# Three of the four sums of weight blocks in a seven-product SwiGLU made by accumulating transfers from GpSimd's queue instead of by VectorE

## The chip, the cores and the metric

The kernel runs on one core of a Trainium2 chip. The metric is device time of the program in microseconds (us), the median of several runs. Times inside the profile are counted from the start of the profiled execution's span. TensorE is PE in the rows (PEld its weight loads), VectorE is DVE, ScalarE is ACT, GpSimd is POOL, SyncE is SP; SP issues the ordinary transfers.

## The reference

A decoder trunk of two layers on 512 tokens of width 1024, in float32. Layer 0 mixes with stick-breaking attention, layer 1 with a dilated attention. Behind each mixer stands a SwiGLU with 2816 hidden columns, and this is the part that matters here:

```python
def _swiglu(h, w_gate, w_up, w_down):
    return (jax.nn.silu(h @ w_gate) * (h @ w_up)) @ w_down
...
    h = h + _swiglu(_rmsnorm(h, norm_ffn[layer]), w_gate[layer], w_up[layer], w_down[layer])
```

## The kernel before, in words

Every matmul runs in three passes: a weight block of 128x512 numbers is split into a high part (`whi`, written by ACT at L306 in a narrower format) and the rest (`wlo`, written by DVE at L307); the activations are split likewise, and high x high, high x rest and rest x high are added up in PSUM. So each weight block costs one load from `wflat` (SP, L243), one ACT instruction and one DVE instruction before PE can use it. `whi` and `wlo` live in a ring of four tiles, `w2hi` and `w2lo` in one of three more; a split may run up to six blocks ahead of PE.

**The SwiGLU.** The 2816 hidden columns are 22 blocks of 128. Blocks 0 and 1 are computed plainly (`gu`). The other twenty go in ten pairs, g = 1 to 10 (`product`, L964). For a pair, gate and up are the rows of a 2x2 block matrix (row: gate or up; column: first or second half of the 1024 inputs), the tokens are its two columns, and seven products P1, P2, P6, P5, P7, P4, P3 replace eight. P1, P2 and P4 take a weight block as it is; P5, P6, P7 and P3 take sums of blocks. With the blocks named w(row, half), and signs folded in elsewhere: s1 = w(1,0)+w(1,1) for P5, s2 = s1+w(0,0) for P6, s3 = w(1,0)+w(0,0) for P7, s4 = s2+w(0,1) for P3. DVE makes them in `split`: s1 at L280, s2 at L281, s3 at L287, s4 at L291, once for each of the twenty blocks of a layer. The tiles `sum` hold s1, s2 and s4, `raw` (or `raw2`) the loaded blocks; s3 is added in place.

Between the products stand the blocks of the down projection (`dn`). It is done in parts: part 0 covers hidden blocks 0 and 1, its eight output blocks follow P7, P4 and P3 of pair 1 (three, three and two of them); the later parts cover four hidden blocks each. A `dn` block accumulates in one of the two PSUM banks `pj`, and DVE adds it to the residual stream `H` (`residual`, L752); the third `dn` in a row can start only when the first one's bank has been read there.

**What sets the order.** The code is written as calls; a scheduler places the instructions on the engines' queues, and each queue is run in order. `weight_stream` lists the blocks to load (`units`) and the splits (`ops`), `Weights.load` issues loads as the `raw` rings allow, `Weights.split` makes sums and splits, and `get` hands a block to PE and splits ahead. Of each queue the head alone can run: what stands behind a waiting instruction waits too.

The entry of the SwiGLU also has VectorE work of its own: the rows' norm (L471 to L482), the token sums for the seven products (`tk`, `XT`, L899 to L914), and the gating of blocks 0 and 1 (L875 to L881, with L877 on GpSimd). GpSimd multiplies `up` by the norm (L951) twice a pair.

Of the kernel before, what the change touches and what calls it, by code (L numbers as in the profile page):

```python
# [79 lines left out]
def weight_stream():  # L80


    units, ops, place = [], [], {}

    def unit(key, width):
        if key not in place:
            place[key] = len(units)
            units.append((key, width))
        return place[key]

    for layer in range(2):
        for kind, i in mixer_order():
            r = (kind, layer, i)
            for j in range(4):
                gain = None
                if layer == 1 and kind == "qk":
                    which, part = (j % 2, j // 2) if crossed(r) else (j // 2, j % 2)
                    gain = ("k", (G_MIX1, G_KV)[which] + 4 * part)
                elif layer == 1 and kind == "v":
                    gain = ("v", G_KV + 2 * j)  # L100
                ops.append((kind, "mix", ("raw", unit((*r, j), 512)), gain))
        for step in ffn_order():
            if step[0] == "gu":
                for j in range(4):
                    ops.append(("gu", "mix", ("raw", unit(("gu", layer, step[1], j), 512)), None))
            elif step[0] == "dn":
                a, b = PARTS[step[1]]
                held = layer == 1 and step[1] == len(PARTS) - 1
                ops.append(("dn", "held" if held else "ffn",
                            ("raw", unit(("dn", layer, *step[1:]), 128 * (b - a))), None))  # L110
            else:
                for i in range(2):
                    f = 2 * step[1] + i
                    w = lambda r, c: unit(("w", layer, f, r, c), 512)
                    what = {"P1": lambda: ("raw", w(0, 0)), "P2": lambda: ("raw", w(0, 1)),
                            "P6": lambda: ("s2", w(1, 0), w(1, 1), w(0, 0)), "P5": lambda: ("s1",),
                            "P7": lambda: ("s3", w(1, 0), w(0, 0)), "P4": lambda: ("raw", w(1, 1)),
                            "P3": lambda: ("s4", w(0, 1))}[step[2]]()
                    ops.append(("pr", "ffn", (*what, i) if what[0][0] == "s" else what, None))
    return units, ops  # L120


def pack_weights(w_qkv_a, w_o_a, w_kv, w_q_b, w_o_b, w_gate, w_up, w_down):

    def cols(m, n):
        k = m.shape[0] // 128
        return m[:, 128 * n:128 * n + 128].reshape(k, 128, 128).transpose(1, 0, 2).reshape(128, -1)

    def block(m, r):
        return m[:, 256 * r:256 * r + 256].reshape(8, 128, 256).transpose(1, 0, 2).reshape(128, -1)  # L130

    wq = [w_qkv_a[0][:, :D], w_q_b[0]]
    wk = [w_qkv_a[0][:, D:2 * D], w_kv[:, :D]]
    wv = [w_qkv_a[0][:, 2 * D:], w_kv[:, D:]]
    wo = [w_o_a[0], w_o_b[0]]
    parts = []
    for key, width in weight_stream()[0]:
        kind, l = key[:2]
        if kind == "qk":
            t = cross(key, [cols(wq[l], key[2]), cols(wk[l], key[2])])[key[3]]  # L140
        elif kind == "v":
            t = block(wv[l], key[2])[:, 512 * key[3]:512 * key[3] + 512]
        elif kind == "o":
            g, q = O_ORDER[4 * key[2] + key[3]]
            t = block(wo[l], g)[:, 512 * q:512 * q + 512]
        elif kind == "gu":
            t = cross(key, [cols(w_gate[l], key[2]), cols(w_up[l], key[2])])[key[3]]
        elif kind == "w":
            _, _, f, r, c = key
# [40 lines left out]
class Weights:  # L190
# [8 lines left out]
    def __init__(self, tc, pool, wflat, gains):  # L199
        self.tc, self.nc, self.pool, self.w, self.gains = tc, tc.nc, pool, wflat, gains  # L200
        self.units, self.ops = weight_stream()
        self.offs = np.concatenate([[0], np.cumsum([128 * n for _, n in self.units])]).tolist()
        last = {}
        for n, op in enumerate(self.ops):
            for u in self.used(op):
# [5 lines left out]
        for n, op in enumerate(self.ops):  # L211
            for u in self.used(op):
                first.setdefault(u, n)

        self.uring, self.oring = [], []
        q = 0
# [11 lines left out]
        self.live = dict.fromkeys(self.size, 0)  # L228
        self.pools = {"raw": pool, "w": pool}
        self.rt, self.wt, self.sums = {}, {}, {}  # L230
        self.nload = self.nsplit = self.nget = 0

    @staticmethod
    def used(op):
        what = op[2]
        return {"raw": what[1:], "s2": what[1:4], "s1": (), "s3": what[1:3], "s4": what[1:2]}[what[0]]

    def load(self):
        u = self.nload
        ring = self.uring[u]  # L240
        _, n = self.units[u]
        t = self.pools[ring].tile([128, 512], F, name=ring, bufs=self.size[ring])
        self.nc.sync.dma_start(t[:, :n], bass.AP(  # L243
            tensor=self.w.tensor, offset=self.w.offset + self.offs[u], ap=[[n, 128], [1, n]]))
        self.rt[u] = t[:, :n]
        self.live[ring] += 1
        self.nload += 1

# [19 lines left out]
    def split(self):  # L268
# [3 lines left out]
        for v in self.used(self.ops[u]):  # L272
            while self.nload <= v:
                self.load()
        r = [self.rt[v] for v in self.used(self.ops[u])]
        if what[0] == "raw":
            v = r[0]
        elif what[0] == "s2":
            s1, s2 = (self.pools["sum"].tile([128, 512], F, name="sum", bufs=4) for _ in range(2))
            nc.vector.tensor_add(s1, r[0], r[1])  # L280
            nc.vector.tensor_add(s2, s1, r[2])  # L281
            self.sums[what[-1]] = (s1, s2)
            v = s2
        elif what[0] == "s1":
            v = self.sums[what[-1]][0]
        elif what[0] == "s3":
            nc.vector.tensor_add(r[0], r[0], r[1])  # L287
            v = r[0]
        else:
            v = self.sums.pop(what[-1])[1]  # L290
            nc.vector.tensor_add(v, v, r[0])  # L291
        n = v.shape[1]
        ring = self.oring[u]
        if ring == "held":
# [10 lines left out]
            nc.gpsimd.tensor_mul(v3, v3, g.unsqueeze(2).to_broadcast([128, n // m, m]))  # L305
        nc.scalar.activation(hi[:, :n], v, AF.Copy)  # L306
        nc.vector.tensor_sub(lo[:, :n], v, hi[:, :n].bitcast(F))  # L307
        self.wt[u] = (hi, lo)
        self.live[ring] += 1
        for v in self.ends.get(u, ()):  # L310
# [5 lines left out]
    def get(self, kind):  # L316
        u = self.nget
        if u and self.oring[u - 1] != "held":
            self.live[self.oring[u - 1]] -= 1
        ahead = self.AHEAD[self.ops[u][1]]  # L320
        while self.nsplit <= min(u + ahead, len(self.ops) - 1) and (
                self.nsplit <= u or self.ready(self.nsplit, u)):
            self.split()
# [5 lines left out]
def trunk(ctx, tc, xg, wflat, cst_d, cs_d, outT):  # L329
# [777 lines left out]


    W.kept = X
    W.kept0 = next(u for u, (key, _) in enumerate(W.units) if key[:3] == ("dn", 1, len(PARTS) - 1))  # L1110
    for c in range(8):
        norm_chunk(c, G_MIX0, None)
    mixer(0, 0, G_FFN0)
# [33 lines left out]
```

## Time and profile before

| what | value |
|---|---|
| runs | 1217.39, 1218.11, 1220.19 us; median 1218.11 |
| profiled execution | 1217.75 us, of which its span 1216.0 us |
| PE busy | 1187.4 us (98%) |
| DVE busy | 1021.9 us (84%) |
| ACT / POOL busy | 698.8 us (57%) / 173.2 us (14%) |
| transfers | 138.30 MB, all issued by SP apart from 1.34 MB of instructions |
| SwiGLU of layer 0 | from about 250 to 602 us in the span |
| SwiGLU of layer 1 | from about 855 to 1200 us |

PE's busy time is modelled from pipelined matmuls. So whether PE waits is read from the idle time ahead of single matmuls and from the pace of a run of them, not from the percentage. An engine other than PE costs time only where a matmul waits for it.

### The profile page before, as it was taken

How to read it: one execution, taken by the hardware profiler on the slowest of the kernel's cores; microseconds unless marked ns; L12 is line 12 of the kernel's file. 1: busy time of each engine (PE TensorE's matmuls, PEld its weight loads, DVE VectorE, ACT ScalarE, POOL GpSimd, SP SyncE). 2: the span in 40 equal slices, each digit the busy share in tenths (PEclk: the TensorE clock that was granted, in tenths of full speed). 3: DMA queues.
4: the chain of work that ended last, by engine and by line, in shares of the span. 5: the costliest groups of instructions: out<-in, count | busy, mean ns of one | idle time of the engine just before them, and what ended most of it. 6: DMA issues, size and time to landing. Idle time of an engine off the chain costs nothing.

```text
span 1216.0 us, 21067 instructions
## 1 busy us (share of the span) xinstructions
PE 1187.4 (98%) x7481; PEld 1060.8 (87%) x7481; DVE 1021.9 (84%) x1833; ACT 698.8 (57%) x1332; POOL 173.2 (14%) x237
## 2 busy tenths in 40 slices
PE   9999999998999999999999999999899999999997
PEld 7989988877999999999788888887789999999996
DVE  6799999899997878787768899788999878787865
ACT  6667676674554444454467677767655454544443
POOL 0000000002100000014225443110011000000111
PEclk9999999999999999999999999999999999999998
DMA  7654644224243323333145556551343433343122
GB/s 262 175 146 115 155 116 119 61 84 159 88 122 94 115 87 114 96 105 87 35 129 144 156 134 176 142 137 53 95 140 105 121 97 112 89 117 88 47 62 70
DMA packets 74361, 138.30 MB, mean 114 GB/s; under 512 B 9617, under 2 KB 13713, under 8 KB 74257
## 3 DMA queue, kind: packets, MB, share of 16 engines
q1 hardware_dynamic: 74256, 136.97, 40.1%
q8 instruction: 59, 0.97, 0.3%
q14 instruction: 46, 0.37, 0.1%
HBM read 106.00 MB, written 2.10 MB: 89 GB/s over the span
## 4 chain that ended last, share of the span: by engine, by line
PE 85%; DVE 6%; DMA 3%; ACT 2%; issue 2%; POOL 1%; SPq 0%; POOLq 0%; DVEq 0%; ACTq 0%
PE pj L388 38%; PE z L388 30%; PE t L388 11%; PE av L388 3%; PE t L704 3%; DMA mov<-hl 1%; DVE wlo L307 1%; DVE H L752 1%; DMA raw<-wflat 1%; DMA rp<-rp 0%; DMA H<-xg 0%; DVE sum L280 0%; DVE w2lo L307 0%; DVE X L422 0%; DVE sum L281 0%
## 5 line engine op out<-in xcount | busy, mean ns | idle before, releaser
L306 ACT ACTIVATE whi<-raw 128x512 fp32r<-128x512 f32 (+1 forms) x290 | 178.2, 620 | 139.1 <-PE pj L388 50.2
L307 DVE TENSOR_TENSOR wlo<-raw,whi 128x512 fp32r<-128x512 f32 (+1 forms) x290 | 203.4, 709 | 25.0 <-ACT whi L306 22.6
L388 PE MATMUL pj<-VO,whi 128*128 128x512 f32 x568 | 180.7, 398 | 0.5 <-DVE H L752 0.4
L388 PE MATMUL pj<-X,whi 128*128 128x512 f32 x512 | 164.9, 401 | 2.6 <-DVE H L752 1.5
L951 POOL TENSOR_TENSOR up<-up,R 128x512 f32<-128x512 f32 x40 | 62.4, 1566 | 495.1 <-DVE up L999 448.8
L388 PEld LDWEIGHTS pj<-VO,whi 128*128 128x128 f32 x568 | 102.4, 189 | 23.1 <-issue 1.2
L388 PEld LDWEIGHTS pj<-X,whi 128*128 128x128 f32 x512 | 92.9, 188 | 23.1 <-issue 1.9
L388 PE MATMUL pj<-VO,wlo 128*128 128x512 f32 x284 | 112.7, 397 | 0.0
L752 DVE TENSOR_TENSOR H<-H,pj 128x512 f32<-128x512 f32 (+1 forms) x120 | 79.3, 664 | 32.5 <-PE pj L388 31.7
L388 PE MATMUL pj<-X,wlo 128*128 128x512 f32 x256 | 101.5, 397 | 0.3 <-DVE wlo L307 0.3
L388 PE MATMUL z<-XT,whi 128*128 128x256 f32 x560 | 99.7, 280 | 0.0
L388 PE MATMUL z<-X,whi 128*128 128x256 f32 (+1 forms) x464 | 96.4, 301 | 1.8 <-DVE s L875 1.8
L306 ACT ACTIVATE w2hi<-raw 128x512 fp32r<-128x512 f32 (+1 forms) x102 | 62.6, 616 | 60.4 <-PE z L388 17.6
L388 PEld LDWEIGHTS z<-XT,whi 128*128 128x128 f32 x560 | 86.2, 189 | 0.7
L388 PE MATMUL pj<-VO,w2hi 128*128 128x512 f32 x264 | 83.1, 396 | 0.4 <-ACT VO L957 0.4
L388 PEld LDWEIGHTS z<-X,whi 128*128 128x128 f32 x464 | 75.1, 189 | 7.0 <-DVE s L875 2.0
L307 DVE TENSOR_TENSOR w2lo<-raw,w2hi 128x512 fp32r<-128x512 f32 (+1 forms) x102 | 70.1, 688 | 11.8 <-ACT w2hi L306 11.5
L388 PE MATMUL z<-XT,wlo 128*128 128x256 f32 x280 | 78.5, 280 | 0.0
L388 PE MATMUL z<-XT,w2hi 128*128 128x256 f32 x400 | 74.9, 287 | 3.6 <-ACT w2hi L306 3.6
L388 PE MATMUL pj<-whi,X 128*128 128x256 f32 x384 | 75.1, 285 | 0.9 <-DVE rp L559 0.9
L388 PE MATMUL z<-X,wlo 128*128 128x256 f32 (+1 forms) x232 | 69.8, 301 | 0.0
L305 POOL TENSOR_TENSOR raw<-raw,H 128x512 f32<-128x512 f32 x48 | 57.9, 1215 | 78.7 <-DMA raw<-wflat 55.6
(207 smaller groups left out, 3029.9 us busy)
## 6 DMA issues: line engine op xcount, KB each, us to landing
raw<-wflat SPq DMA_DIRECT2D x384, 256.0 KB, 2.8
mov<-hl SPq DMA_DIRECT2D x64, 256.0 KB, 4.5
sta<-hl SPq DMA_DIRECT2D x64, 128.0 KB, 2.4
rp<-rp SPq DMA_DIRECT2D x56, 64.0 KB, 2.0
raw<-wflat SPq DMA_DIRECT2D x16, 128.0 KB, 2.6
H<-xg SPq DMA_DIRECT2D x7, 256.0 KB, 5.4
outT<-H SPq DMA_DIRECT2D x2, 512.0 KB, 3.1
CS<-cs SPq DMA_DIRECT2D x1, 512.0 KB, 3.4
```

Of the source, the lines that this page charges most:

```text
L305: nc.gpsimd.tensor_mul(v3, v3, g.unsqueeze(2).to_broadcast([128, n // m, m]))
L306: nc.scalar.activation(hi[:, :n], v, AF.Copy)
L307: nc.vector.tensor_sub(lo[:, :n], v, hi[:, :n].bitcast(F))
L388: pe.matmul(out, a, b, start=start, stop=stop, skip_group_check=True)
L704: pe.transpose(b[:, o:o + 128], pr[i][:, 128 * c:128 * c + 128], idf)
L752: dve.tensor_add(H[:, n, e], H[:, n, e], p[:, e])
L951: pool.tensor_mul(two(u), two(u), r)
```

## The change

Of the four sums only s2 stays on VectorE. s1 and s3 are made while loading: a block is loaded into its `raw` tile as before, and then a second transfer, issued from GpSimd's queue with an adding write, adds another block from memory to the tile. w(1,0) is therefore loaded twice, for s1 and for s3. s4 is made the same way: w(0,1) is added by a transfer to the tile that holds s2, once s2 has been split. `Weights.adds` lists the transfers still to issue; `add(n)` issues those that belong to splits below n, and `get` calls it with a lead of four splits over the splitting itself. `used` no longer keeps w(1,1) and w(0,1) for the sums, and each sum takes one `sum` tile where s1 and s2 took two.

```diff
-                    w = lambda r, c: unit(("w", layer, f, r, c), 512)
-                    what = {"P1": lambda: ("raw", w(0, 0)), "P2": lambda: ("raw", w(0, 1)),
-                            "P6": lambda: ("s2", w(1, 0), w(1, 1), w(0, 0)), "P5": lambda: ("s1",),
-                            "P7": lambda: ("s3", w(1, 0), w(0, 0)), "P4": lambda: ("raw", w(1, 1)),
-                            "P3": lambda: ("s4", w(0, 1))}[step[2]]()
-                    ops.append(("pr", "ffn", (*what, i) if what[0][0] == "s" else what, None))
+                    k = lambda r, c: ("w", layer, f, r, c)
+                    w = lambda *p: unit(k(*p[0]), 512, k(*p[1]) if len(p) > 1 else None)
+                    what = {"P1": lambda: ("raw", w((0, 0))), "P2": lambda: ("raw", w((0, 1))),
+                            "P6": lambda: ("s2", w((1, 0), (1, 1)), w((0, 0)), k(0, 1), i),
+                            "P5": lambda: ("raw", w((1, 0), (1, 1))),
+                            "P7": lambda: ("raw", w((1, 0), (0, 0))), "P4": lambda: ("raw", w((1, 1))),
+                            "P3": lambda: ("s4", i)}[step[2]]()
+                    ops.append(("pr", "ffn", what, None))
...
+    def add(self, n):
+
+        while self.adds and self.adds[0][0] < n:
+            _, t, key = self.adds.pop(0)
+            self.nc.gpsimd.dma_start(t, self.source(key, 512), accum_op=OP.add)
...
         self.rt[u] = t[:, :n]
+        if added:
+            self.adds.append((self.first[u], t[:, :n], added))
+            self.adds.sort(key=lambda x: x[0])
...
+        self.add(u + 1)
         r = [self.rt[v] for v in self.used(self.ops[u])]
         if what[0] == "raw":
             v = r[0]
         elif what[0] == "s2":
-            s1, s2 = (self.pools["sum"].tile([128, 512], F, name="sum", bufs=4) for _ in range(2))
-            nc.vector.tensor_add(s1, r[0], r[1])
-            nc.vector.tensor_add(s2, s1, r[2])
-            self.sums[what[-1]] = (s1, s2)
-            v = s2
-        elif what[0] == "s1":
-            v = self.sums[what[-1]][0]
-        elif what[0] == "s3":
-            nc.vector.tensor_add(r[0], r[0], r[1])
-            v = r[0]
+            v = self.pools["sum"].tile([128, 512], F, name="sum", bufs=4)
+            nc.vector.tensor_add(v, r[0], r[1])
+            self.sums[what[4]] = v
         else:
-            v = self.sums.pop(what[-1])[1]
-            nc.vector.tensor_add(v, v, r[0])
+            v = self.sums.pop(what[1])
...
+        if what[0] == "s2":
+
+            self.adds.append((u + 8, v, what[3]))
+            self.adds.sort(key=lambda x: x[0])
...
         ahead = self.AHEAD[self.ops[u][1]]
+        self.add(u + ahead + 4)
```

The changed kernel's lines are 11 to 16 higher: L306 becomes L317, L307 becomes L318, L752 becomes L768, L878 becomes L894. The sum that stays is L299, the accumulating transfer L252.

VectorE's queue at the entry of layer 0's SwiGLU before, from the gating of block 1 (L878) to the rests of the first products of pair 1. `sum_3286` and `sum_3294` are s1, `sum_3287` and `sum_3295` s2, `raw_3076` becomes s3:

```order
L878 TENSOR_TENSOR s_3254<-s_3254,z_3175 128x512
L881 TENSOR_TENSOR VO_63<-s_3153,VO_63 128x512
L280 TENSOR_TENSOR sum_3286<-raw_3076,raw_3106 128x512
L881 TENSOR_TENSOR VO_63<-s_3254,VO_63 128x512
L281 TENSOR_TENSOR sum_3287<-sum_3286,raw_2982 128x512
L280 TENSOR_TENSOR sum_3294<-raw_3112,raw_3180 128x512
L287 TENSOR_TENSOR raw_3076<-raw_3076,raw_2982 128x512
L307 TENSOR_TENSOR w2lo_3291<-sum_3287,w2hi_3290 128x512
L281 TENSOR_TENSOR sum_3295<-sum_3294,raw_3012 128x512
L307 TENSOR_TENSOR wlo_3319<-sum_3294,whi_3318 128x512
L307 TENSOR_TENSOR wlo_3339<-raw_3076,whi_3338 128x512
L307 TENSOR_TENSOR w2lo_3299<-sum_3295,w2hi_3298 128x512
```

The same place now. `raw_3076` and `raw_3106` hold s1 when they are read, `sum_3294` and `sum_3302` are s2:

```order
L894 TENSOR_TENSOR s_3256<-s_3256,z_3175 128x512
L897 TENSOR_TENSOR VO_63<-s_3153,VO_63 128x512
L299 TENSOR_TENSOR sum_3294<-raw_3076,raw_2982 128x512
L897 TENSOR_TENSOR VO_63<-s_3256,VO_63 128x512
L299 TENSOR_TENSOR sum_3302<-raw_3106,raw_3012 128x512
L318 TENSOR_TENSOR w2lo_3297<-sum_3294,w2hi_3296 128x512
L318 TENSOR_TENSOR wlo_3329<-raw_3106,whi_3328 128x512
L318 TENSOR_TENSOR w2lo_3305<-sum_3302,w2hi_3304 128x512
L318 TENSOR_TENSOR w2lo_3311<-raw_3076,w2hi_3310 128x512
L318 TENSOR_TENSOR wlo_3350<-raw_3112,whi_3349 128x512
L318 TENSOR_TENSOR wlo_3369<-raw_3180,whi_3368 128x512
```

The first s2 is ready after one addition in the place of two, and three additions no longer stand ahead of the rests.

A little later on VectorE's queue before, around the first `dn` blocks of part 0 (L752 adds them to `H`). `sum_3657` is s1 of pair 2:

```order
L291 TENSOR_TENSOR sum_3295<-sum_3295,raw_3070 128x512
L307 TENSOR_TENSOR wlo_3490<-raw2_3273,whi_3489 128x256
L999 TENSOR_TENSOR up_3486<-up_3485,z_3416 128x512
L752 TENSOR_TENSOR H_61<-H_61,pj_3493 128x512
L307 TENSOR_TENSOR wlo_3502<-raw2_3275,whi_3501 128x256
L280 TENSOR_TENSOR sum_3657<-raw_3437,raw_3455 128x512
L752 TENSOR_TENSOR H_61<-H_61,pj_3505 128x512
L307 TENSOR_TENSOR w2lo_3515<-sum_3287,w2hi_3514 128x512
L752 TENSOR_TENSOR H_61<-H_61,pj_3520 128x512
```

The same place now. `sum_3665` and `sum_3683` are s2 of pair 2, and read `raw_3353` and `raw_3372` after the transfers that add to these:

```order
L318 TENSOR_TENSOR wlo_3466<-raw2_3275,whi_3465 128x512
L318 TENSOR_TENSOR wlo_3484<-raw2_3277,whi_3483 128x256
L299 TENSOR_TENSOR sum_3665<-raw_3353,raw_3300 128x512
L299 TENSOR_TENSOR sum_3683<-raw_3372,raw_3308 128x512
L1015 TENSOR_TENSOR up_3502<-up_3501,z_3428 128x512
L318 TENSOR_TENSOR wlo_3506<-raw2_3279,whi_3505 128x256
L768 TENSOR_TENSOR H_61<-H_61,pj_3511 128x512
L318 TENSOR_TENSOR wlo_3520<-raw2_3281,whi_3519 128x256
L768 TENSOR_TENSOR H_61<-H_61,pj_3525 128x512
```

Both sums of pair 2 stand ahead of the first `dn` block's reading, each behind a load and an accumulating transfer.

GpSimd's queue at the entry now. Before, only the multiplications stood there, L439 and twice L877, which are L455 and L893 here:

```order
L455 TENSOR_TENSOR ACC_65<-H_61 128x512
L252 DMA raw_3076<-wflat 128x512
L252 DMA raw_3106<-wflat 128x512
L252 DMA raw_3112<-wflat 128x512
L252 DMA raw_3180<-wflat 128x512
L893 TENSOR_TENSOR s_3153<-s_3153,R_64 128x512
L893 TENSOR_TENSOR s_3256<-s_3256,R_64 128x512
L252 DMA sum_3294<-wflat 128x512
L252 DMA sum_3302<-wflat 128x512
L252 DMA raw_3353<-wflat 128x512
L252 DMA raw_3372<-wflat 128x512
```

The first four transfers stand ahead of the gating's multiplications; those for pair 2 stand behind the two for s4 of pair 1. PE's queue is the same in both kernels apart from four matmuls that change places with a neighbour.

## Rows read from the trace of the kernel before

**Rows 1.** The page, busy time by engine (us, share, instructions).

```profile
PE 1187.4 (98%) x7481; PEld 1060.8 (87%) x7481; DVE 1021.9 (84%) x1833; ACT 698.8 (57%) x1332; POOL 173.2 (14%) x237
```

**Rows 2.** Windows: us; busy PE, PEld, DVE, ACT, POOL; granted clock; DMA share; GB/s.

```profile
302.00:560.00 258.00, 257.93 (x1833) 241.70 (x1834) 217.99 (x343) 127.32 (x217) 31.39 (x22) 1.00 0.36 105
930.00:1160.00 230.00, 230.00 (x1624) 214.86 (x1623) 191.67 (x303) 113.10 (x194) 24.25 (x16) 1.00 0.35 96
```

**Rows 3.** Chain of waits in pair 3 of layer 0: start, us, what.

```profile
349.44 2.84 PE t L388 x24
352.28 2.81 PE pj L388 x12
```

**Rows 4.** Instructions by line, VectorE's sums: count, busy us, mean ns, idle before.

```profile
L281 DVE TENSOR_TENSOR sum<-sum,raw 128x512 f32<-128x512 f32 x40 | 27.5, 687 | 0.6
L291 DVE TENSOR_TENSOR sum<-sum,raw 128x512 f32<-128x512 f32 x40 | 27.5, 687 | 0.1
```

**Rows 5.** Timeline of PE, entry of layer 0's SwiGLU: start, us [idle, releaser].

```profile
275.34 0.50 PE L388 MATMUL z<-X,whi 128*128 128x256 f32 x2 [1.78 <-DVE s L875]
281.60 0.51 PE L388 MATMUL z<-XT,w2hi 128*128 128x256 f32 x2 [2.00 <-ACT w2hi L306]
282.74 0.38 PE L388 MATMUL z<-XT,w2lo 128*128 128x256 f32 x1 [0.64 <-DVE w2lo L307]
284.04 0.99 PE L388 MATMUL z<-XT,w2hi 128*128 128x256 f32 x4
285.15 0.38 PE L388 MATMUL z<-XT,w2lo 128*128 128x256 f32 x1
```

**Rows 6.** Timeline of VectorE, the same stretch.

```profile
278.99 0.68 DVE L280 TENSOR_TENSOR sum<-raw 128x512 f32<-128x512 f32 x1
280.20 0.68 DVE L281 TENSOR_TENSOR sum<-sum,raw 128x512 f32<-128x512 f32 x1
280.80 0.68 DVE L280 TENSOR_TENSOR sum<-raw 128x512 f32<-128x512 f32 x1
282.00 0.68 DVE L307 TENSOR_TENSOR w2lo<-sum,w2hi 128x512 fp32r<-128x512 f32 x1
284.41 1.28 DVE L307 TENSOR_TENSOR w2lo<-sum,w2hi 128x512 fp32r<-128x512 f32 x2
```

**Rows 7.** Timeline of ScalarE, the same stretch.

```profile
280.91 0.63 ACT L306 ACTIVATE w2hi<-sum 128x512 fp32r<-128x512 f32 x1 [1.29 <-DVE sum L281]
```

**Rows 8.** Timeline of PE, entry of layer 1's SwiGLU.

```profile
878.15 0.77 PE L388 MATMUL t<-X,whi 128*128 128x256 f32 x2 [3.11 <-DVE s L875]
884.30 0.50 PE L388 MATMUL z<-XT,w2hi 128*128 128x256 f32 x2 [1.56 <-ACT w2hi L306]
885.44 0.58 PE L388 MATMUL z<-XT,w2lo 128*128 128x256 f32 x1 [0.64 <-DVE w2lo L307]
```

**Rows 9.** Windows of 2 us at that entry.

```profile
878.00:880.00 2.00, 1.85 (x9) 1.88 (x9) 1.45 (x3) 1.26 (x2) 1.78 (x2) 0.53 0.57 184
886.00:888.00 2.00, 2.00 (x12) 2.00 (x11) 2.00 (x4) 1.34 (x3) 0.00 (x0) 0.50 0.43 115
890.00:892.00 2.00, 2.00 (x19) 2.00 (x19) 1.79 (x4) 2.00 (x6) 0.00 (x0) 1.00 0.79 188
```

**Rows 10.** Timeline of PE, the first and third `dn` block of layer 0's part 0.

```profile
291.88 0.63 PE L388 MATMUL pj<-VO,whi 128*128 128x512 f32 x2
294.67 0.63 PE L388 MATMUL pj<-VO,w2hi 128*128 128x512 f32 x2
```

**Rows 11.** Timeline of VectorE, the first of these blocks added to H.

```profile
293.51 0.68 DVE L752 TENSOR_TENSOR H<-H,pj 128x512 f32<-128x512 f32 x1
```

**Rows 12.** Transfers by line: queue, count, KB each, median us from issue to landing.

```profile
raw<-wflat SPq DMA_DIRECT2D x384, 256.0 KB, 2.8
cst<-cst SPq DMA_DIRECT2D x1, 256.0 KB, 5.6
```

**Rows 13.** Window of the start, columns as in Rows 2.

```profile
0.00:30.00 30.00, 27.20 (x152) 21.38 (x153) 18.91 (x33) 18.12 (x33) 1.62 (x8) 1.00 0.78 266
```

More of the change, by code (lines that the diff above doesn't have):

```diff
@@ L83, in weight_stream, with unit @@
     units, ops, place = [], [], {}
[L85 to L89, printed above, removed]
+    def unit(key, width, added=None):
+        if (key, added) not in place:
+            place[key, added] = len(units)
+            units.append((key, width, added))
+        return place[key, added]
     for layer in range(2):
@@ L136, in pack_weights @@
     parts = []
-    for key, width in weight_stream()[0]:
+    for key, width, _ in weight_stream()[0]:
         kind, l = key[:2]
@@ L201, in __init__ @@
         self.units, self.ops = weight_stream()
-        self.offs = np.concatenate([[0], np.cumsum([128 * n for _, n in self.units])]).tolist()
+        self.offs = np.concatenate([[0], np.cumsum([128 * n for _, n, _ in self.units])]).tolist()
+        self.at = {}
+        for (key, _, _), at in zip(self.units, self.offs):
+            self.at.setdefault(key, at)
         last = {}
@@ L213, in __init__ @@
                 first.setdefault(u, n)
+        self.first = first
         self.uring, self.oring = [], []
@@ L230, in __init__ @@
         self.rt, self.wt, self.sums = {}, {}, {}
+        self.adds = []
         self.nload = self.nsplit = self.nget = 0
@@ L235, in used, with source @@
         what = op[2]
-        return {"raw": what[1:], "s2": what[1:4], "s1": (), "s3": what[1:3], "s4": what[1:2]}[what[0]]
+        return {"raw": what[1:], "s2": what[1:3], "s4": ()}[what[0]]
+    def source(self, key, n):
+        return bass.AP(tensor=self.w.tensor, offset=self.w.offset + self.at[key], ap=[[n, 128], [1, n]])
+    def add(self, n):
+        while self.adds and self.adds[0][0] < n:
+            _, t, key = self.adds.pop(0)
+            self.nc.gpsimd.dma_start(t, self.source(key, 512), accum_op=OP.add)
     def load(self):
@@ L240, in load @@
         ring = self.uring[u]
-        _, n = self.units[u]
+        key, n, added = self.units[u]
         t = self.pools[ring].tile([128, 512], F, name=ring, bufs=self.size[ring])
-        self.nc.sync.dma_start(t[:, :n], bass.AP(
-            tensor=self.w.tensor, offset=self.w.offset + self.offs[u], ap=[[n, 128], [1, n]]))
+        self.nc.sync.dma_start(t[:, :n], self.source(key, n))
         self.rt[u] = t[:, :n]
+        if added:
+            self.adds.append((self.first[u], t[:, :n], added))
+            self.adds.sort(key=lambda x: x[0])
         self.live[ring] += 1
@@ L1109, in trunk @@
     W.kept = X
-    W.kept0 = next(u for u, (key, _) in enumerate(W.units) if key[:3] == ("dn", 1, len(PARTS) - 1))
+    W.kept0 = next(u for u, (key, *_) in enumerate(W.units) if key[:3] == ("dn", 1, len(PARTS) - 1))
     for c in range(8):
```

## The prediction

> **What bounds the kernel now.** I read the busy times first: PE 98%, VectorE 84% [rows 1]. A share over the whole span doesn't say where the 16% and the 2% lie, so the next view is windows over the two SwiGLU stages. From pair 2 on PE is busy for 257.93 of 258 us in layer 0 and 230.00 of 230 in layer 1 [rows 2]. The chain of waits confirms it at single steps: a product (24 matmuls) takes 2.84 us, a `dn` block (12 matmuls) 2.81, one behind the other with nothing between [rows 3]. VectorE is busy there for 217.99 of 258 us and no matmul waits for it. So whatever VectorE gets back in these stretches is worth nothing.
>
> The timeline of PE then shows where VectorE does decide: at the entry of each SwiGLU. In layer 0 PE idles for 1.78 us for the gating (L875), 2.00 us until ScalarE has the first high part of P6, 0.64 us until VectorE has its rest, and again ahead of the rest at 285.15, since the four matmuls from 284.04 last 4 x 0.118 = 0.47 us: 0.64 us more [rows 5]. Behind the 2.00 us stands VectorE's queue: L280 from 278.99, another instruction, L281 from 280.20 to 280.88, then ScalarE's copy from 280.91 to 281.54 [rows 6, 7]. Layer 1 shows the same waits, 1.56 and 0.64 us, behind one of 3.11 us for the gating [rows 8]. There the granted clock is also down, 0.53 just after the 3.11 us and 0.50 at 886, which is the lower of the two levels (1.2 GHz) [rows 9].
>
> **The change part by part.**
>
> *Removed from VectorE.* Three additions for each of 40 blocks: 120 x 0.687 us [rows 4] = 82 us of busy time. Nearly all of it lies beside a saturated PE and is hidden by it. On the path are only those ahead of P6 at the two entries. In the new order L299 takes the place that L280 had, 278.99 to 279.67. ScalarE's copy of 0.63 us then ends at 280.33 and PE starts at 280.40 instead of 281.60: 1.20 us. The rest of the first block moves from fifth to third behind that sum: it starts at 280.80 instead of 282.00, 1.20 us earlier as well, so the 0.64 us behind it stays and isn't gained twice. The second block's rest starts at 282.00 instead of behind 284.41, and the last 0.64 us go. Sum: 1.84 us an entry. I take the same for layer 1, whose rows show the same pattern.
>
> *The clock in layer 1.* At the lower level PE started 12 matmuls in 2 us, at the full one 19 [rows 9], so a stretch at 0.50 costs 37% of its busy part. The second such stretch has about 3 us of busy time, some 1.1 us. In layer 0 waits of 1.78 and 2.00 us within 8 us left the clock up, in layer 1 a wait of 3.11 us came ahead of the fall. With the second wait shortened by 1.20 us the second stretch may go; half of 1.1 us is counted, bounds 0 and 1.1.
>
> *Added: 120 accumulating transfers and 40 more loads.* The trace has no transfer from GpSimd's queue and no adding one. Let L be the time from the landing of the plain load below it to its own landing. From below: 2.8 us, a load of the same 256 KB [rows 12]. From above: 5.6 us, the slowest median of a 256 KB load, plus 0.8 for reading the bytes twice and 0.6 behind the other one that is issued with it, 7.0 us. The 0.8 is 256 KB at 266/0.78 = 341 GB/s [rows 13]. I take the middle of 3.6 (a load with its bytes read twice) and 5.6, so 4.6 us.
>
> For the first pair the transfers are early. The blocks of s1 and s3 go to places that are free at 255 to 262 us, 17 us ahead of their use; GpSimd has nothing else there. For s4 the queue gives 11 us or more between the issue and ScalarE's use, for s1 and s3 of later pairs 20 us and more ahead of ScalarE. What is early is VectorE's own use: L299 for the next pair stands right behind its transfers.
>
> *The added wait.* At the entry this is tight. L299 for pair 2 stands ahead of `up` (L1015), a rest and the first reading of a `dn` block (L768). The load below it goes to the place that the fifth instruction from 280.80 on, `wlo_3350`, frees: 280.80 + 4 x 0.60 + 0.68 = 283.9 (0.60 is the spacing from 280.20 to 280.80 [rows 6]), the second load 0.6 later, landed at 287.3 with the 2.8 of [rows 12]. Then the sum starts at 287.3 + L, and 0.60, 0.60, 0.35 (half a tile) and 0.68 later the first `dn` block is in H: 289.5 + L. The third `dn` block needs its bank. Before, VectorE read it at 293.51 to 294.19 and PE went on at 294.67 [rows 10, 11]; the entry being 1.84 us shorter, it wants it at 292.83. So PE waits for L - 3.3 us: nothing at 2.8, 1.3 at 4.6, 3.7 at 7.0. That is queued behind L299, and the third `dn` block is late next.
>
> *The same wait in later pairs.* There the `dn` blocks stand singly between products of 2.84 us, and the rests (L318) are made up to six splits ahead. A wait of some us on VectorE, which has 16% idle time before [rows 2] and 4 us less to do per pair, is made good ahead of PE: nothing is charged. This cover is gone if a wait lasts longer than about five splits, 5 x 1.42 = 7 us.
>
> *The transfer engines.* A pair with four `dn` blocks lasts 7 x 2.84 + 4 x 2.81 = 31 us [rows 3]. Its 14 loads need 14 x 0.77 = 11 us of all 16 engines, which leaves 20 us, 3.4 us for each of six accumulating transfers. At two reads, 1.5 us, they fit.
>
> *Sum.* Layer 0: 1.84 - 1.3 = 0.5 us. Layer 1: 1.84 - 1.3 + 0.55 = 1.1. Together 1.6 us off the profiled execution's 1217.75 (its span of 1216.0 and 1.75 around it), 1216.15. The median of the runs shown is 1218.11, 0.36 above that execution: 1216.5 us.
>
> **The Trainium skill beside it.** No row shows a transfer from GpSimd's queue. "DMA: Bandwidth & Descriptors", section "Anatomy of one DMA — SWDGE (gpsimd) path", gives 2.0 us and the bytes over 436 GB/s for one; that would be an estimate of 2.6 us here and the quick rival below. The same page's table "Rules for kernel authors" says that nothing holds an accumulating transfer's destination meanwhile, so that the earlier transfer's completion has to be waited for; that is the two steps in a row, load and addition, that the sum charges. "Collectives: The Full Stack", section "The bandwidth ceiling", has an adding copy at about half the rate of a plain one, because it reads twice; by it 1.5 us of the engines would stand, as in the sum.
>
> **The rivals.**
>
> 1. *The transfers are quick.* L at 3.3 us or less: no wait at the `dn` blocks, both 1.84 us remain, and the clock in layer 1 stays up. 1218.11 - 3.7 - 1.1 = 1213.3. For it: a plain load takes 2.8 and the queue is idle. Against: two reads, and descriptors made by GpSimd. This is where the first page named above would put it.
>
> 2. *VectorE stands behind its own sum (slower).* L at 5 us or more: from 5.1 on the wait at the third `dn` block eats the 1.84 us. At 7.0 it is 3.7 us, longer than the 3.11 us after which the clock fell, so 1.1 us more for a stretch at the lower level: 2 x (3.7 - 1.84 + 1.1) = 5.9, 1224.0. For it: loads that start together take 5.6 us, and the loads of pairs 1 and 2 start within a few us of these transfers. Against: pair 2's loads now start one by one as places come free.
>
> 3. *The transfer engines, or GpSimd's issuing, become the bound.* If an addition takes all engines over 3.4 us, each us above that costs 6 us a pair; at 4 us some 0.6 x 120 = 72 us less what is ahead, 1285. Against: that is over four times a plain load's 0.77.
>
> That the change does nothing at all, because PE is saturated, is contained in the forecast: it is why the 82 us become 1.6.
>
> **How the numbers follow.** Forecast (L between 3.5 and 5.6): 47%, own range 1214.5 to 1218.8. Rival 1: 26%. Rival 2: 20%. Rival 3: 7%. A measurement of this kernel can't tell less than 0.2%, 2.4 us, from no change. Faster than 1215.7: rival 1 and a little of the forecast, 33%. Slower than 1220.5: most of rival 2 and all of rival 3, 24%. Within: 43%. The range from 1213 to 1224 leaves out rival 3, the slow end of rival 2 and the quick end of rival 1.
>
> **What would show it.** VectorE's busy time falls by about 80 us and ScalarE's hardly moves. In layer 0 PE's wait ahead of the first P6 falls from 2.00 to about 0.8 us, and the two of 0.64 become one. At the third `dn` block of part 0 PE waits for L768 by about 1.3 us, with L299 ahead of it on VectorE waiting for a transfer. From pair 2 on PE is as full as before. Wrong would be: matmuls that wait between 310 and 560 us, a DMA share near 1 there, or no wait of L299 at all; and the sum would be off in its largest term if L is outside 3.5 to 5.6.

## The result and the profile after

The changed kernel takes 1233.98 us (median of 4 runs, 1233.62 to 1234.31) against 1218.01: a ratio of 1.0128 to the kernel before, 95% interval [1.011, 1.0145]. It is 16 us slower; the forecast was 1216.5, its range ended at 1224.

First the page of the changed kernel: busy time by engine as in [rows 1], two DMA queues (packets, MB, share of 16 engines' span; q0 is GpSimd's, q1 SP's), and the issues of 256 KB as in [rows 12].

```profile
PE 1191.1 (97%) x7481; PEld 1064.8 (86%) x7481; DVE 948.5 (77%) x1713; ACT 697.5 (57%) x1332; POOL 275.4 (22%) x357
...
q1 hardware_dynamic: 80016, 147.46, 41.2%
q0 software_dynamic: 17280, 31.46, 16.6%
...
raw<-wflat SPq DMA_DIRECT2D x424, 256.0 KB, 3.2
raw<-wflat POOLq DMA_DIRECT2D x80, 256.0 KB, 5.5
```

VectorE has 73 us less to do (about 120 x 0.60, the spacing of its instructions in a row), and nothing came of it. An adding transfer holds the engines for 16.6% of 1231.8 us / 120 = 1.70 us, a load of SP for 41.2% x 1231.8 / (147.46 MB / 262144 bytes) = 0.90.

Windows of the changed kernel, columns as in [rows 2]: the two stretches from pair 2 on, the 14 us around the first `dn` blocks of layer 0, and three windows of 2 us behind these.

```profile
310.00:560.00 250.00, 250.00 (x1784) 234.57 (x1783) 179.73 (x284) 122.86 (x210) 66.94 (x66) 1.00 0.74 175
...
946.00:1176.00 230.00, 230.00 (x1623) 214.94 (x1622) 163.19 (x258) 112.35 (x194) 61.02 (x60) 1.00 0.70 167
...
282.00:296.00 14.00, 9.72 (x71) 8.85 (x69) 5.93 (x12) 5.21 (x11) 4.12 (x5) 0.92 1.06 278
...
298.00:300.00 2.00, 1.21 (x3) 1.01 (x4) 2.00 (x4) 0.00 (x0) 1.27 (x1) 0.50 0.38 108
...
302.00:304.00 2.00, 2.00 (x11) 2.00 (x11) 1.05 (x2) 0.00 (x0) 0.00 (x0) 0.50 0.00 0
304.00:306.00 2.00, 2.00 (x17) 1.91 (x16) 0.78 (x2) 0.83 (x2) 0.00 (x0) 1.00 0.05 5
```

From pair 2 on PE is as full as in [rows 2]: 250 of 250 us, 230 of 230, with a DMA share of 0.7 in the place of 0.36. The loss is at the entry: from 282 to 296 us the transfer engines are saturated (1.06; the same window of the kernel before has 0.63), PE is busy for 9.72 of 14 us, and behind it PE runs at the lower clock (0.50) until 304.

The timeline of PE, which answers to [rows 5, 8 and 10]:

```profile
274.16 0.52 PE L404 MATMUL z<-X,whi 128*128 128x256 f32 x2 [1.79 <-DVE s L891]
...
279.70 0.50 PE L404 MATMUL z<-XT,w2hi 128*128 128x256 f32 x2 [1.23 <-ACT s L1002]
280.36 0.39 PE L404 MATMUL z<-XT,w2lo 128*128 128x256 f32 x1 [0.16 <-DVE w2lo L318]
...
288.77 0.63 PE L404 MATMUL pj<-VO,whi 128*128 128x512 f32 x2
...
298.79 1.22 PE L404 MATMUL pj<-VO,w2hi 128*128 128x512 f32 x2 [7.07 <-DVE H L768]
...
886.12 0.47 PE L404 MATMUL t<-X,whi 128*128 128x256 f32 x2 [3.11 <-ACT s L1002]
...
891.07 0.79 PE L404 MATMUL z<-XT,w2hi 128*128 128x256 f32 x2 [1.03 <-ACT w2hi L317]
...
911.24 1.22 PE L404 MATMUL pj<-VO,w2hi 128*128 128x512 f32 x2 [5.17 <-DVE H L768]
```

The same matmul's start, before and after, gives the account. 275.34 to 274.16: 1.18 us ahead (in the program's first 10 us, which the change does not touch). First `dn` block, 291.88 to 288.77: 3.11 ahead, so the entry gained 1.93. Third `dn` block, 294.67 to 298.79: 4.12 behind, 7.23 us lost in one place. A product of pair 3, 349.44 in [rows 3], stands here in the chain of waits:

```profile
356.27 2.84 PE t L404 x24
```

That is 6.83 behind: 2.7 us more, of which most is the lower clock until 304. Layer 1 begins 7.97 behind (878.15 to 886.12), gains 1.20 (884.30 to 891.07), loses that again to the lower clock by its first `dn` block, waits 5.17 us at its third, and the execution ends 15.8 behind.

VectorE's timeline says what the third `dn` block waited for; it answers to [rows 11]:

```profile
287.89 0.42 DVE L318 TENSOR_TENSOR wlo<-raw,whi 128x256 fp32r<-128x256 f32 x1 [0.51 <-ACT whi L317]
295.24 0.69 DVE L299 TENSOR_TENSOR sum<-raw 128x512 f32<-128x512 f32 x1 [6.92 <-DMA raw<-wflat]
296.52 0.69 DVE L299 TENSOR_TENSOR sum<-raw 128x512 f32<-128x512 f32 x1 [0.59 <-DMA raw<-wflat]
297.12 0.68 DVE L1015 TENSOR_TENSOR up<-up,z 128x512 f32<-128x512 f32 x1
297.72 0.42 DVE L318 TENSOR_TENSOR wlo<-raw,whi 128x256 fp32r<-128x256 f32 x1
298.06 0.68 DVE L768 TENSOR_TENSOR H<-H,pj 128x512 f32<-128x512 f32 x1
```

VectorE stands idle for 6.92 us with L299 at the head of its queue, and the reading of the first `dn` block, possible since that block ended at about 290.3, stands four places behind. The load under the first sum was issued at 282.74 and landed at 288.68; the transfer that adds to it was issued at 289.24 and landed at 295.21. The transfers issued meanwhile (SP's from 282 to 288.5, GpSimd's from 289 to 292.5, and for comparison one that GpSimd issued alone at 308), median us to landing last:

```profile
raw<-wflat SPq DMA_DIRECT2D x9, 256.0 KB, 6.3
...
raw<-wflat POOLq DMA_DIRECT2D x4, 256.0 KB, 6.2
...
raw<-wflat POOLq DMA_DIRECT2D x1, 256.0 KB, 4.2
```

### The profile page after: what moved, and what is told of

Read it like the earlier page. It is cut to its first block, busy times and chain, and to the rows that moved or that the text cites. A ratio compares the mean times of both kernels' runs of the same rounds, so it can differ in the third digit from the quotient of the medians.

```text
span 1231.8 us, 21327 instructions
## 1 busy us (share of the span) xinstructions
PE 1191.1 (97%) x7481; PEld 1064.8 (86%) x7481; DVE 948.5 (77%) x1713; ACT 697.5 (57%) x1332; POOL 275.4 (22%) x357
## 3 DMA queue, kind: packets, MB, share of 16 engines
q1 hardware_dynamic: 80016, 147.46, 41.2%
q0 software_dynamic: 17280, 31.46, 16.6%
## 4 chain that ended last, share of the span: by engine, by line
PE 86%; DVE 5%; DMA 3%; issue 3%; ACT 1%; POOL 1%; SPq 0%; POOLq 0%; DVEq 0%; ACTq 0%
PE pj L404 39%; PE z L404 29%; PE t L404 12%; PE av L404 3%; PE t L720 3%; DMA raw<-wflat 2%; DVE wlo L318 1%; DVE H L768 1%; DMA mov<-hl 1%; DVE ACC L459 0%; POOL H L1075 0%; DVE X L438 0%; POOL s L893 0%; ACT X L437 0%; DMA rp<-rp 0%
## 5 line engine op out<-in xcount | busy, mean ns | idle before, releaser
L317 ACT ACTIVATE whi<-raw 128x512 fp32r<-128x512 f32 (+1 forms) x322 | 197.6, 621 | 144.6 <-PE pj L404 45.2
L318 DVE TENSOR_TENSOR wlo<-raw,whi 128x512 fp32r<-128x512 f32 (+1 forms) x322 | 224.7, 707 | 37.5 <-ACT whi L317 36.8
L252 POOL DMA_DIRECT2D raw<-wflat x80 | 71.2, 948 | 214.8 <-DMA raw<-wflat 88.2
L317 ACT ACTIVATE w2hi<-raw 128x512 fp32r<-128x512 f32 (+1 forms) x110 | 67.4, 617 | 69.7 <-PE z L404 25.7
L768 DVE TENSOR_TENSOR H<-H,pj 128x512 f32<-128x512 f32 (+1 forms) x120 | 79.3, 664 | 32.6 <-PE pj L404 32.0
L318 DVE TENSOR_TENSOR w2lo<-raw,w2hi 128x512 fp32r<-128x512 f32 (+1 forms) x110 | 74.9, 687 | 18.6 <-ACT w2hi L317 17.8
L316 POOL TENSOR_TENSOR raw<-raw,H 128x512 f32<-128x512 f32 x48 | 57.5, 1206 | 83.1 <-DMA raw<-wflat 51.9
```

The lines of the kernel that those rows point to most:

```text
L252: self.nc.gpsimd.dma_start(t, self.source(key, 512), accum_op=OP.add)
L768: dve.tensor_add(H[:, n, e], H[:, n, e], p[:, e])
```

## The experiments

Theory A: VectorE's queue stands at a sum for a transfer, and that alone costs. Rivals: the traffic slows everything (B), or the loss is elsewhere (C). All runs are compared with runs of the kernel before on the same chip (medians 1218.98 to 1219.77 us); the ratios, not the times, are compared from run to run.

**Two places for the sums in the place of four.**

```diff
-            v = self.pools["sum"].tile([128, 512], F, name="sum", bufs=4)
+            v = self.pools["sum"].tile([128, 512], F, name="sum", bufs=2)
```

> The ring of `sum` tiles has two places in the place of four. By that the sums L299 for pair 2 have to wait for a place, and stand on VectorE's queue behind the third reading of a `dn` block (L768) where they stood ahead of the first; all loads and accumulating transfers are issued in the same order as in the changed kernel. Theory A (what costs is VectorE standing at the head of its queue for the transfers into the two sums): both waits for L768 go, 7.07 us in layer 0 and 5.17 in layer 1, with the stretches at the lower clock behind them, so that the curve of PE's delay loses its steps of 10.1 and 7.5 us: 1233.98 - 17.6 = 1216.4 us, and the 1.9 us gained ahead of the first P6 remain. Rival B (the transfers load the engines, the plain loads land in 6 us where they took 2.8, and all that follows is late whoever waits for it): half of the loss or more stays, 1225 us or above, with PE waiting for splits (L317, L318) at the same place. Rival C (the loss is GpSimd's or the order's, elsewhere): no change, 1234 us.

1223.93 us, ratio 1.0037 [1.0025, 1.0049]. Some eleven of the 16 us are gone, and the third `dn` block no longer waits. VectorE, then PE:

```profile
297.28 0.69 DVE L299 TENSOR_TENSOR sum<-raw 128x512 f32<-128x512 f32 x1 [0.76 <-DVE w2lo L318]
...
299.22 0.69 DVE L299 TENSOR_TENSOR sum<-raw 128x512 f32<-128x512 f32 x1 [0.91 <-DVE w2lo L318]
...
302.61 0.68 DVE L768 TENSOR_TENSOR H<-H,pj 128x512 f32<-128x512 f32 x1
```

```profile
303.34 1.22 PE L404 MATMUL pj<-VO,whi 128*128 128x512 f32 x2 [4.01 <-DVE H L768]
```

The sums now stand ahead of the fourth reading, and the sixth `dn` block waits 4.01 us for that one. A's mechanism holds, its number (1216.4) does not: the wait was moved along the queue. VectorE idles there for 0.76 and 0.91 us, until the transfers under the sums land at 297.20 and 299.14 (the view names an instruction of VectorE that had ended by then); the rest it loses beside GpSimd, whose product it waits for (1.15 us), and whose multiplication stretches an instruction ahead of the sums to 2.31 us (see the last section). Loads and transfers are as slow as before.

**Additions left out.**

```diff
-            self.nc.gpsimd.dma_start(t, self.source(key, 512), accum_op=OP.add)
+            pass
```

> The accumulating transfers are left out, so that s1, s3 and s4 each lack one block; the 40 additional plain loads and the three fewer additions on VectorE stay. It tells what the rest of the change is worth, and whether the plain loads at the entry are slow by themselves. Theory A: no wait of L299 for a transfer, PE does not wait at the third `dn` block, 1216 us (the gain of about 1.9 us an entry, part of it lost again to the clock in layer 1), as the kernel with two sum tiles. If the plain loads take 2.8 us here at 281 to 289 us, the additions slow them; if they still take about 6, it is the ten loads that are issued within 8 us. Rival B: 1214 to 1216 as well, but then the kernel with two sum tiles stays far above it. Rival C (additional loads or the order cost the 16 us): 1228 us or more.

1214.88 us, 0.9964 [0.9952, 0.9976]: the gain without its price. C falls. Transfers issued from 282 to 289 us here:

```profile
raw<-wflat SPq DMA_DIRECT2D x9, 256.0 KB, 3.9
```

3.9 us in the place of 6.3: it is the transfers that slow the loads behind them. (Whether by adding or by being there: plain writes, below, leave 5.7.)

For the next kernels each sum can be made either way, by a function that `weight_stream` asks; pairs and sums are named as in the text (L299 is L309 for s1 and L311 for s2 there, L768 is L787, L318 is L337):

```diff
+def by_transfer(s, layer, g):
+    return not (s == "s1" and g == 2)
...
+                            "P5": lambda: ("raw", *s1()) if by("s1") else ("s1", i),
```

**s1 of pair 2 on VectorE** (the condition above).

> s1 of pair 2 alone, in both layers, is made by VectorE again, four of 120 transfers; the other 116 stay. Theory A: VectorE's sums of pair 2 now wait for two plain loads and no transfer. If these land at about 289.7 us as in the changed kernel, the first L768 ends some 3.8 us later, at 293.5, and PE waits 1.8 us for it where it waited 7.07: about 1233.98 - 2 x 6.5 - 2 for the clock = 1219 us; 1216 if the loads land earlier. Rival B: 116 transfers load the engines as 120 did, so 1228 us or more. Rival C: no change, 1234.

1222.31 us, 1.0029 [1.0018, 1.0041], where A had 1219 at most. No sum waits for a transfer, yet PE waits 3.02 us at the third `dn` block, because the plain loads land at 291, not 289.7. A alone does not explain that; B is part of it.

**Pair 1 only** (`return g == 1`), and **s1 and s3 of pair 1 only** (`return g == 1 and s in ("s1", "s3")`).

> Only pair 1 of each layer makes s1, s3 and s4 by transfer (12 transfers), pairs 2 to 10 are as before the change. Theory A: the 1.9 us at each entry remain, the sums of pair 2 wait for plain loads alone: 1215 to 1219 us, like the kernel with s1 of pair 2 on VectorE, since transfers from pair 3 on cost PE nothing. Rival B: the slow loads at the entry come from the many transfers about, so this one is clearly below the kernel that keeps 116 of them, at 1215 against 1228. Rival C: the cost is spread over the pairs; about 1216 here.

> Only s1 and s3 of pair 1 come by transfer (8 transfers, issued at 257 to 267 us), s4 and all later pairs are made by VectorE. Against the kernel with all three sums of pair 1 by transfer (1223.34) it lacks four transfers, the s4 of pair 1 in both layers. Theory A2: without these the loads issued from 281.7 on land in about 3 to 4.3 us as with no transfers at all, no wait at the third `dn` block, the gain at both entries stays: 1215 us. Rival F (slow loads come from the earlier transfers or from the new order of the loads): 1221 or more.

1223.34 us, 1.0024 [1.0012, 1.0036], and 1216.41 us, 0.9971 [0.9962, 0.998]. In the first no theory had more than 1219; the second came out near A2's 1215. The two differ by s4 of pair 1: two transfers a layer, issued from 281 us on, or two additions on VectorE. Loads issued from 282 to 289 us, first with them, then without:

```profile
raw<-wflat SPq DMA_DIRECT2D x8, 256.0 KB, 7.1
```

```profile
raw<-wflat SPq DMA_DIRECT2D x9, 256.0 KB, 4.3
```

The first sum of pair 2 (L309) and the first reading of a `dn` block (L787) on VectorE, first with the s4 transfers, then without:

```profile
291.80 0.69 DVE L309 TENSOR_TENSOR sum<-raw 128x512 f32<-128x512 f32 x1 [4.93 <-DMA raw<-wflat]
...
295.49 0.68 DVE L787 TENSOR_TENSOR H<-H,pj 128x512 f32<-128x512 f32 x1
```

```profile
291.32 0.68 DVE L787 TENSOR_TENSOR H<-H,pj 128x512 f32<-128x512 f32 x1
...
293.56 0.69 DVE L309 TENSOR_TENSOR sum<-raw 128x512 f32<-128x512 f32 x1 [0.50 <-DMA raw<-wflat]
```

So the 7 us between the two (6.5 by the ratios) have two causes that this pair of runs does not separate. The load that the sum waits for is slow with the s4 transfers: issued at 284.1, it takes 7.6 us, where without additions one issued at 284.0 took 3.6 and PE waited 0.67 us. And the order differs: with s4 on VectorE the place for that load comes free only at 289.3, the load lands later still (293.5), but the sum now stands behind the first reading, and PE does not wait at the third `dn` block. Some 3.5 us more of the first kernel's profile are lost from 640 to 735 us, where the edit changes nothing. s1 and s3 of pair 1, issued from 257 to 267 us, cost nothing.

**Plain writes in the place of additions.**

```diff
-            self.nc.gpsimd.dma_start(t, self.source(key, 512), accum_op=OP.add)
+            self.nc.gpsimd.dma_start(t, self.source(key, 512))
```

> All 120 transfers from GpSimd's queue stay in their places and orders, but write without adding, so that s1, s3 and s4 hold the last block alone. It tells the adding from the queue. Theory A2 (an adding transfer holds the engines for 16.6% of 1231.8 us / 120 = 1.70 us where a plain load of the same size holds them for 41.2% of 1231.8 / 562 = 0.90; at the entries the two s4 transfers of pair 1, issued at 280.6 and 281.8, so push back the loads behind them and the transfers behind these): here the loads land some 1.6 us earlier and each transfer too, the wait at the third `dn` block falls from 7.07 to about 3.6 us, and the time to 1223 us (1220 to 1226). Rival D (it is the descriptors that GpSimd writes, 0.86 us each, and its queue): 1234 us, as with the addition. Rival E (the adding makes all of it): as with no transfers at all, 1215.

1228.71 us, 1.0075 [1.006, 1.0089]: outside the range of A2, between D and E. Its page and PE's timeline:

```profile
q0 software_dynamic: 9600, 31.46, 8.1%
...
raw<-wflat POOLq DMA_DIRECT2D x80, 256.0 KB, 3.3
```

```profile
297.59 1.22 PE L404 MATMUL pj<-VO,w2hi 128*128 128x512 f32 x2 [5.64 <-DVE H L768]
```

The adding doubles the engines' time (8.1% of 1227.4 / 120 = 0.83 us without it), and some 6 of the 16 us are its share (by the ratios). The rest is there with any transfer in its place: a second step behind the load, in a crowd. The loads issued from 282 to 289 us still took 5.7 us, and the transfer under the first sum, issued at 288.37, took 6.0, as with the addition.

**s4 of pair 1 on VectorE** (`return not (s == "s4" and g == 1)`), and **that and s1 of pair 2** (`return (s, g) not in (("s4", 1), ("s1", 2))`).

> Everything by transfer but s4 of pair 1, which VectorE makes (4 of 120 transfers taken out). The place into which s1 of pair 2 is loaded comes free later now, and its sums L299 stand one on each side of the third reading of a `dn` block. Theory A2: the loads are quick, but VectorE still stands at L299 for a load (landed at about 294) and a transfer behind it of 4.6 to 6 us, so until 299 or 300; the fifth `dn` block waits for the third one's bank for some 3 to 4 us, and the clock may fall: 1221 to 1224 us. Rival G (the four s4 transfers are all of the cost): 1215 us.

> s4 of pair 1 and s1 of pair 2 are made by VectorE, 112 of 120 transfers stay. Theory A2: the loads at the entry are quick and no sum of pair 2 waits for a transfer: both entries keep their gain, and the other 112 transfers cost nothing, since PE is full there and the splits are far ahead: 1215 to 1217 us, as with 8 transfers. Rival H (the transfers of pair 2 and 3 slow the loads and splits behind the entry): 1220 or more, with a wait of PE at 295 to 310 us.

1228.47 us, 1.008 [1.0066, 1.0095], and 1223.22 us, 1.0039 [1.0024, 1.0054]. In the first the chain of load and transfer is 6.18 us of idle VectorE again and PE waits 4.25 and 1.72 us: G falls, the direction was right and the price too low. In the second I expected 1216, and the time is H's. VectorE, GpSimd, and the closing DRAIN of the program (ns, min/median/max):

```profile
292.92 2.52 DVE L309 TENSOR_TENSOR sum<-raw 128x512 f32<-128x512 f32 x1 [1.26 <-DMA raw<-wflat]
```

```profile
293.26 1.62 POOL L986 TENSOR_TENSOR up<-up,R 128x512 f32<-128x512 f32 x1
```

```profile
L1177 POOLq DRAIN  x3: 40/102/9195, 1210.0 to 1219.7; - x3
```

The sum of pair 2 waits 1.26 us for its load and then takes 2.52 us beside GpSimd's multiplication, where 0.68 is usual, and PE waits 2.44 us at the sixth `dn` block. And the program ends late, with no engine busy after 1213: the DRAIN, which closes GpSimd's queue, lasts until 1219.2. In this profile PE's last matmul starts at 1209.10, 0.2 us behind the kernel before (1208.94), and 11.0 us follow it in the place of 7.0. So the wait at the `dn` block eats the entries' gain, and what lies above the kernel before is the closing, which H did not have.

**s1 of pair 2 alone** (`return g == 2 and s == "s1"`), four transfers.

> s1 of pair 2 alone comes by transfer (4 of 120), all else as before the change. Those are the transfers that VectorE waited for in the changed kernel. Here the loads below them are issued at 286 to 288 us, behind a busier VectorE, and the two sums stand behind the third reading of a `dn` block. Theory A3 (the price is not in the transfer but in where the sum stands on VectorE's queue and in the crowd of loads and transfers it shares the engines with): load landed at about 290.5, transfer 5 to 6 us later, sums at 296 to 299 us, the fourth reading at about 301 as before: PE waits no more than 1 us, 1218 to 1220.5 us. Rival I (a chain of load and transfer costs at this place whatever else is there): a wait of 3 us or more an entry, 1224 us or more.

1233.28 us, 1.0113 [1.0097, 1.0129]: a clear miss. I had taken the load of another block; those of s1 land at 294.7 and 295.4. VectorE with a multiplication of GpSimd, PE, and the two transfers (issued from 295 to 297 us); L316 makes s3 of pair 2:

```profile
296.12 3.01 DVE L316 TENSOR_TENSOR raw<-raw 128x512 f32<-128x512 f32 x1 [0.41 <-DMA raw<-wflat]
...
296.62 1.95 POOL L986 TENSOR_TENSOR up<-up,R 128x512 f32<-128x512 f32 x1
...
302.15 0.69 DVE L311 TENSOR_TENSOR sum<-raw 128x512 f32<-128x512 f32 x1 [0.62 <-DMA raw<-wflat]
...
303.36 0.69 DVE L311 TENSOR_TENSOR sum<-raw 128x512 f32<-128x512 f32 x1 [0.18 <-DMA raw<-wflat]
...
304.90 1.75 DVE L316 TENSOR_TENSOR raw<-raw 128x512 f32<-128x512 f32 x1
```

```profile
307.39 1.19 PE L423 MATMUL pj<-VO,whi 128*128 128x512 f32 x2 [4.34 <-DVE H L787]
```

```profile
raw<-wflat POOLq DMA_DIRECT2D x2, 256.0 KB, 7.0
```

The time is rival I's, its reason is not shown. PE waits 4.3 and 4.4 us at the two entries, for the fourth reading, with the lower clock behind each. But in layer 0 VectorE stands for the two transfers for only 0.62 and 0.18 us. 3.4 us come from the two L316, which stand ahead of the same reading and take 3.01 and 1.75 us beside GpSimd's multiplications, where 0.68 is usual. The clock also fell ahead of the transfers (0.50 from 282 to 288 us, 1.00 in the kernel before), which cost 1.6 us, and 6.8 us more are lost in this run's profile from 640 to 735 us, in layer 1's mixer, where the edit changes nothing (the other profiles lose 0.1 to 3.7 us there against the kernel before). That part stays open, and with it what four transfers cost at this place by themselves.

**s1 of pair 1 alone** (`return g == 1 and s == "s1"`), twice.

> s1 of pair 1 alone comes by transfer (4 of 120). Theory A3: it is these four that shorten the entry, since each takes one addition from ahead of the first P6 and nothing waits for the transfers, issued 20 us ahead; the two s3 additions (L316) that stay stand behind the first rests, 1.2 us of VectorE that PE does not wait for. So 1215.5 to 1217 us, as with s1 and s3 by transfer (1216.41). Rival J (the s3 additions ahead of P7's rest count too): 1217.5 to 1218.5 us.

> The kernel with s1 of pair 1 alone by transfer, once more, so that the one before stands beside it: 1215 to 1217 us, 0.997 of the kernel before. If the earlier 0.9967 was chance, the ratio is 1 within 0.1%.

1215.60 us, 0.9967 [0.9954, 0.9979], and 1215.05 us, 0.9961 [0.9946, 0.9975]: faster than both kernels, with four transfers, issued 20 us ahead of their use. The gain at the entry is that of the additions left out; J falls.

**Pairs 4 to 10 as well** (`return g >= 4 or (s, g) == ("s1", 1)`).

> s1 of pair 1 and all three sums of pairs 4 to 10 come by transfer (88 of 120); s3 and s4 of pair 1 and all sums of pairs 2 and 3 are made by VectorE. The order on VectorE is that of the kernel with s1 of pair 1 alone until well behind the entry. Theory A (the loss sits at the entry alone; later the transfers are hidden, though each holds the transfer engines 1.7 us, since `dn` blocks stand singly there and the splits are ahead): within 1 us of that kernel, about 1215.6 us. Rival K (each later transfer costs something that the entry's loss has covered up): 1218 us or more.

1217.00 us, 0.9981 [0.9972, 0.999], beside 1215.05 on the same chip. A window and the closing DRAIN:

```profile
302.00:560.00 258.00, 257.71 (x1839) 241.70 (x1838) 192.61 (x302) 126.82 (x217) 66.80 (x63) 1.00 0.65 161
```

```profile
L1177 POOLq DRAIN  x3: 40/102/7237, 1207.5 to 1215.3; - x3
```

PE is as full as without the 84 later transfers (257.66 of 258 there), and its last matmul starts no later (1206.8 us against 1207.7 and 1208.7 in the two runs with s1 of pair 1 alone). The closing is longer: 8.8 us from that start to the end of the span, against 7.0. So the later transfers cost PE nothing, as A said, and in this profile the program's end some 1.7 us, which neither theory had.

## Why the prediction was wrong

**Right.** That PE is full from pair 2 on and the 73 us of VectorE are worth nothing. The place and the mechanism of the loss: the third `dn` block, L768 behind L299, L299 behind a transfer. The transfer engines' time for an addition, 1.5 us forecast and 1.70 measured. Rival 2 was the right story, at 20%.

**Right by luck.** The gain at the entry of layer 0, 1.84 us forecast and 1.93 measured up to the first `dn` block. Its terms were 1.20 for the start of P6, nothing for the first rest and 0.64 for the second; they came out at 0.72, 0.48 and 0.73. ScalarE's copy for P6 ended at 279.16, as forecast (280.33, less the 1.18 us by which this execution is ahead), but the first P6 waited on until 279.70, for ScalarE's next instruction, which reads P1's result:

```profile
279.06 0.58 ACT L1002 ACTIVATE s<-z 128x512 f32<-128x512 f32 x1
```

**The step that failed** is the price in "the added wait": "Then the sum starts at 287.3 + L", and "PE waits for L - 3.3 us: nothing at 2.8, 1.3 at 4.6, 3.7 at 7.0". The sum started at 295.24. This execution is 1.18 us ahead from its first 10 us on, so in the forecast's times that is 296.42, or 287.3 + 9.1. From the forecast's 1.3 to 7.07 us lead these terms: 2.6 because the load landed at 288.68, 289.86 in the forecast's times; 1.9 because L, from there to the transfer's landing, was 6.5 in the place of 4.6 (outside 3.5 to 5.6, which the prediction had named as the sign of a wrong term); 0.6 because the working counted one instruction too few between the first sum and the reading (two sums, `up` and a rest stand there); 0.7 because the second sum waited for a transfer of its own. Sum: 7.1. PE itself was at the third `dn` block when the forecast had it there (291.72, or 292.90; 292.83 was forecast).

**Why load and transfer were late.** The prediction took 2.8 us for the load [rows 12], a median over the whole program, and charged the crowd to L alone. At this place it was 5.9, with a median of 6.3 about it. Rows for a crowd were in the trace of before: its own window from 282 to 296 us has a DMA share of 0.63 with one load about every us, and the loads issued from 284 to 294 us took 4.4 us on the median. (The 5.6 us that stood for loads that start together is one load of constants.) "At two reads, 1.5 us, they fit" is true of a pair of 31 us and false of 14 us that hold some ten loads, two s4 transfers and four more. That s4's own use was far off was right; that its transfers stand in the way of the loads behind them was not thought of (7.6 us for a load behind them, 3.6 without transfers). Nor was it that taking s4 off VectorE frees a place earlier and so sets the sums of pair 2 ahead of the first reading, where before the change they stood behind it. L for a single transfer on an idle queue was well guessed: 4.2 us to land, and some 0.5 between the load's landing and the issue.

**The clock** was priced at 1.1 us for layer 1 alone. After the 7.07 us PE ran at 0.50 in layer 0 too. In layer 1 it fell at another place than in [rows 9]: after the same 3.11 us it stayed up, and it was down behind the next waits:

```profile
886.00:888.00 2.00, 1.88 (x14) 1.72 (x14) 1.47 (x2) 1.27 (x3) 1.79 (x2) 1.00 1.01 313
...
892.00:894.00 2.00, 1.78 (x8) 1.78 (x9) 2.00 (x5) 1.06 (x3) 1.22 (x2) 0.50 0.70 204
```

So the forecast's 1.84 + 0.55 us at that entry came out at nothing up to the first `dn` block. The kernel without additions gained 2.5 us on the same stretch.

**The range** ended at 1224, with 7.0 us as the upper bound of L, which held (6.5), and the load held at 2.8, which did not. Two steps in a chain that share one resource have to be bounded together.

The Trainium skill's fit in "DMA: Bandwidth & Descriptors", section "Anatomy of one DMA — SWDGE (gpsimd) path" (estimate 2.6 us), is near the plain transfers from GpSimd's queue (3.3 us on the median) and far from the adding ones: 4.2 alone, 5.5 on the median. The measurement decides here.

## What to carry to other kernels

Work that is taken from an engine and given to a transfer still makes that engine wait, if its next use of the result stands early in its queue: look at what stands behind it there, and price load, issue and transfer as a chain, at the load of the very microseconds in which it runs. Look also at what the scheduler does with the order: a place that comes free earlier can set a waiting instruction ahead of one that PE needs. A few transfers, issued long ahead of their use and where the transfer engines are idle, gave the whole gain (4 of 120, 0.996 of the time before); each of the others was at best hidden.

## What the runs showed of the hardware that was not expected

- GpSimd's closing DRAIN grows with transfers from its queue, not evenly: 2.19 us with none, 2.54 with 4, 2.87 with 8, 3.19 with 12, 3.36 with 120 and 3.03 with 116, but 7.24 with 88 and 9.20 with 112. In the last two it ends after all else and sets the end of the program. What decides between 3 and 9 us was not tried.
- An addition of VectorE took 2.52 us, and another 3.01, in the place of 0.68 beside a multiplication on GpSimd. Beside GpSimd's issuing of transfers it did not stretch: of the changed kernel's 128x512 TENSOR_TENSOR instructions on VectorE the 196 that overlap only that took 0.683 us on the mean, 711 beside nothing on GpSimd 0.685, and 124 that overlap arithmetic there 0.845 (from the starts and ends in the trace). The Trainium skill's "SBUF — State Buffer", section "SBUF: two separate sides", has such a lock between a VectorE operation with two inputs from SBUF and a GpSimd operation that reads SBUF; the trace agrees for single instructions.
- An adding write holds the transfer engines twice as long as a plain one from the same queue: 1.70 us against 0.83 for 256 KB. It moves them in 144 packets, the plain one in 80 (17280 and 9600 for 120 transfers, on the two pages).
